# Output projection of an encoder block: another order of two products, and four instructions tied behind others

## The chip, the cores and the metric

The kernel runs on one core of a Trainium2 chip. A core has five engines that run side by side, each through its own queue in order: TensorE (PE, matrix products, with its weight loads listed as PEld), VectorE (DVE), ScalarE (ACT), GpSimd (POOL) and SyncE (SP). DMAs are issued from the queues of SP, POOL and ACT. Semaphores hold an instruction back until what it reads or overwrites is ready; what stands behind it in the same queue waits with it. The metric is the time of one execution on the device in microseconds (us); shorter is better.

## The reference: one encoder block in float32

The block has 512 tokens of width 1024. Three mixers (a bidirectional mLSTM, neighbourhood attention, cross attention into 256 memory tokens) are merged by sigmoid gates; then follow the output projection with its residual, and a convolutional GLU:

```python
h = rms_norm(x, mix_norm_g[l])
...
merged = g_ml * (y_ml @ w_br_ml[l]) + g_na * (y_na @ w_br_na[l]) + g_xa * (y_xa @ w_br_xa[l])
x = x + merged @ w_out[l]
x = x + conv_glu_ffn(rms_norm(x, ffn_norm_g[l]), w_ffn_up[l], w_ffn_conv[l], b_ffn_conv[l], w_ffn_down[l])
...
return rms_norm(x, final_norm_g)
```

The change lies in the line `x = x + merged @ w_out[l]`, with the sums of squares for the `rms_norm` of the line after it. `merged` is 512 x 1024 and `w_out` is 1024 x 1024.

## The kernel before

**Precision.** Every float32 operand of a product is split in two float32r tiles: ACT copies it (the high half), and DVE subtracts that copy from the source (the low half). `mm3` (L223 to L226) makes a product of three matmuls: high by high (L224), high by low (L225), low by high (L226). The third is the first that reads the low half of the left operand.

**The projection by seven products.** The projection (L1370 to L1460) cuts `merged` and `w_out` in quarters and uses a scheme with seven products instead of eight. `ORDER_O` names them in the order in which they run: p1, p2, p5, p6, p3, p7, p4. Each product has four steps k of two token halves t, so 4 x 2 x 3 = 24 matmuls of 128 x 512. The four quarters a11, a21, a12, a22 of the merged activations lie in `mg` (L1313). Some products read a quarter as it is (p1: a11, p2: a12, p4: a22), the others a quarter that was overwritten with a sum or difference: `early` (L1116) makes a21 = a21 - a22 and a11 = a21 - a11 after the last branch gate (L1367 and L1368); `operand` (L1123) makes the two sums for p3 (L1129 and L1130).

`operand` converts one left operand: it takes a unit (one of 15 wide buffers, `NU`), copies to the high half on ACT (L1132) and subtracts for the low half on DVE (L1136). Operands of a later product are converted at step k = 1 of the product before it (L1439).

`o_raw` (L1214) loads the right operand of a product in two halves by SP's queue, from `wout` or from `tout`, where sums of quarters of the weights were put earlier. `o_split` (L1229) converts each half: high half on ACT (L1234), low half on DVE (L1235). p6 and p7 (places 3 and 5, `RING_O`) use the three small buffers that the stream of all weights (L160, split at L184 and L185) goes through; the others use units.

**Sums of the products.** A product fills two PSUM banks, and there are two such pairs, used in turn (`wide`, L1375): a product can start once the product two places before it has been read. The reading is `add` in `wide_adder` (L1173):

- p1: ACT copies it into Q (L1180).
- p2: DVE writes p2 + Q into cell (0, 0) of x (L1182), and `residual` (L1169) issues a DMA from POOL's queue that adds the rows of the input to the cell in place (L1171).
- p5: ACT copies it into the cells (0, 1) and (1, 1) (L1186), and each gets its residual by such a DMA.
- p6: Q = p6 + Q (L1189). p3: added to cell (0, 1) (L1191). p7: Q = Q - p7 (L1193). p4: added to cell (1, 0) at the end (L1163).
- With no name and a cell, Q is added to the cell or subtracted from it (L1175).

A cell is two tiles of 128 tokens by 512 columns: cell (0, 0) is the first column half of tokens 0 to 255, cell (0, 1) the second column half of the same tokens.

**What comes after.** `squares` (L1197) makes a sum of squares over half a row of a token tile on ACT (L1199). `normed` (L1387) takes the mean of two of them (L1209, DVE), the power on POOL (L1204), and scales the rows (L1395, ACT). `turn` (L1403) transposes the scaled rows on PE (L1410); its call for tokens 0 to 255 stands at step 2 of p4, and its results, split at L230 and L231, feed the up projection of the GLU.

**What sets the order.** The loop at L1433 writes the program down; the list `todo` (L1424) names the step of a product at which each of the reading parts is written. From this a planner makes the queue of each engine: it keeps the written order as a priority, but puts an instruction that it thinks ready ahead of one that it thinks not ready yet, by its own cost model. `tc.issue_after(ins)` ties what is written within it behind `ins` on the engine of `ins`.

Of the kernel before, what the change touches and what calls it, by code (L numbers as in the profile page):

```python
# [11 lines left out]
F32 = mybir.dt.float32  # L12
F32R = mybir.dt.float32r
AF = mybir.ActivationFunctionType
ALU = mybir.AluOpType
# [3 lines left out]
S = 512  # L19
D = 1024  # L20
# [5 lines left out]
HF = FT // 2  # L26
TK = 6
ORDER = ("p1", "p5", "p6", "p3", "p7", "p2", "p4")
ORDER_O = ("p1", "p2", "p5", "p6", "p3", "p7", "p4")
RING_O = (3, 5)  # L30
OBL = [(n, hf) for n in ORDER_O for hf in range(2)]
NU = 15
# [70 lines left out]
def hybrid_block(ctx, tc, xg, xT, xtok, memT, wflat, wout, wdn, vecs, gbias, nabias, out):  # L103
    nc = tc.nc
    V, A, G, PE, SY = nc.vector, nc.scalar, nc.gpsimd, nc.tensor, nc.sync
# [17 lines left out]
    def unit(dt=F32):  # L123
        return up.tile([P, UNIT], dt, tag="unit", name=nm("u"))

    def scr(n=512):
        return sp.tile([P, S], F32, tag="scr", name=nm("s"))[:, :n]

    def tiny(n):
        return tp.tile([P, 32], F32, tag="tiny", name=nm("y"), bufs=12)[:, :n]  # L130
# [18 lines left out]
    st = {"raw": 0, "split": 0, "last": BINDEX[("ua", 0)][0] - 1}  # L149
# [148 lines left out]
    for i in range(2):  # L298
        t = cp.tile([P, 514], F32, name=f"pad{i}")
# [812 lines left out]
    def quads(pair, nk):  # L1112
        v = [u[:, :nk * S].rearrange("p (k s) -> p k s", k=nk) for u in pair]
        return v[0][:, :, :HS], v[0][:, :, HS:], v[1][:, :, :HS], v[1][:, :, HS:]

    def early(q, i):  # L1116
        a11, a21, a12, a22 = q
        if i == 0:
            V.tensor_tensor(a21, a21, a22, op=ALU.subtract)
        else:  # L1120
            V.tensor_tensor(a11, a21, a11, op=ALU.subtract)

    def operand(name, q, nk, scale=1.0):  # L1123
        a11, a21, a12, a22 = q
        u = unit(F32R)
        h, l = u[:, :nk * HS], u[:, 1024:1024 + nk * HS]
        r3 = lambda t: t.rearrange("p (k s) -> p k s", s=HS)
        if name == "p3":
            V.tensor_tensor(a21, a22, a11, op=ALU.add)  # L1129
            V.tensor_tensor(a11, a12, a11, op=ALU.add)  # L1130
        src = {"p1": a11, "p5": a21, "p6": a11, "p3": a11, "p7": a21, "p2": a12, "p4": a22}[name]
        A.activation(r3(h), src, AF.Copy, scale=scale)  # L1132
        if scale == 1.0:
            V.tensor_tensor(r3(l), src, r3(h).bitcast(F32), op=ALU.subtract)  # L1134
        else:
            V.scalar_tensor_tensor(r3(l), src, scale, r3(h).bitcast(F32), op0=ALU.mult, op1=ALU.subtract)  # L1136
        return h, l
# [4 lines left out]
    def cells(c):  # L1142
        return xtu[c[0]][:, :2 * D].rearrange("p (t n) -> p t n", t=2)[:, :, c[1] * S:(c[1] + 1) * S]
# [23 lines left out]
    def wide_adder(banks, Q):  # L1167
# [26 lines left out]

        return add

    def squares(t, n, c0, c1):  # L1197
        s = tiny(1)
        A.activation(scr(c1 - c0), xt[t][:, c0:c1], AF.Square, scale=D ** -0.5, accum_out=s)  # L1199
        n.append(s)  # L1200
# [11 lines left out]
    oraw, osp, oops, opair = [], [], {}, []  # L1212

    def o_raw(n):  # L1214
        while len(oraw) < min(n, len(OBL)):
            name, hf = OBL[len(oraw)]
            src, q = {"p1": (wout, B11), "p5": (tout, T1), "p6": (tout, T2), "p3": (wout, B22), "p7": (tout, T3),
                      "p2": (wout, B21), "p4": (tout, T4)}[name]
            n_ = ORDER_O.index(name)
            if n_ in RING_O:  # L1220
# [8 lines left out]
    def o_split(n):  # L1229
        while len(osp) < min(n, len(OBL)):  # L1230
            r = oraw[len(osp)]
            u = unit(F32R)
            h, l = u[:, :2 * S], u[:, 2 * S:4 * S]
            A.activation(h, r, AF.Copy)  # L1234
            V.tensor_tensor(l, r, h.bitcast(F32), op=ALU.subtract)  # L1235
            osp.append((h, l))

    gens = []
# [29 lines left out]
    for f in range(4):  # L1268
        ps = paced(("o", f), RN if f else RB)
        t = scr()  # L1270
# [31 lines left out]
    for f in range(4):  # L1302
        ps = paced(("naq", f), RN)
        V.tensor_tensor(nq[:, f * S:(f + 1) * S].rearrange("p (b r c) -> p b r c", r=ROWS, b=4), rv(ps), rv(rb),
                        op=ALU.mult)
# [15 lines left out]
    for br in range(3):  # L1321
# [19 lines left out]
        for fp in range(4):  # L1341
# [7 lines left out]
            if br == 2:  # L1349
                if fp == 2:  # L1350
                    mq = quads(mg, 4)
# [31 lines left out]
    add = wide_adder(obank, Qo)  # L1383
    part = [[] for _ in range(NT)]
    zs = {}

    def normed(t):  # L1387
        col = power(mean(part[t]))
        zs[t] = []
        for hf in range(2):  # L1390
            z = tp.tile([P, S], F32, tag="H", name=nm("z"), bufs=4)
            if t > 1 and hf:
                V.tensor_scalar(z, xt[t][:, hf * S:(hf + 1) * S], col, None, op0=ALU.mult)
            else:
                A.activation(z, xt[t][:, hf * S:(hf + 1) * S], AF.Copy, scale=col)  # L1395
            zs[t].append(z)

    def features():
        h2 = [unit(F32R) for _ in range(4)]
        HH.extend(h2[k // 4 * 2][:, (k % 4) * S:(k % 4 + 1) * S] for k in range(KT))  # L1400
        HL.extend(h2[k // 4 * 2 + 1][:, (k % 4) * S:(k % 4 + 1) * S] for k in range(KT))
# [14 lines left out]
    xtu = [unit(), unit()]  # L1416
    xt = [xtu[t // 2][:, t % 2 * D:(t % 2 + 1) * D] for t in range(NT)]
    SY.dma_start(cells((1, 0)), xtok[2 * P:, :S].rearrange("(t p) n -> p t n", p=P))
    oops["p2"] = operand("p2", mq, 4, 0.5)
    early(mq, 0)  # L1420
    oops["p5"] = operand("p5", mq, 4, 0.5)
    early(mq, 1)
    todo = {}
    for name, k, fn in (  # L1424
            ("p2", 1, lambda: add("p1")), ("p5", 1, lambda: add("p2")), ("p6", 1, lambda: add("p5")),
            ("p3", 1, lambda: add("p6")), ("p3", 3, lambda: [squares(t, part[t], 0, S) for t in range(2)]),
            ("p7", 0, lambda: (add("p3"), add("", (0, 1)), [squares(t, part[t], S, D) for t in range(2)])),
            ("p7", 1, lambda: [normed(t) for t in range(2)]),
            ("p4", 0, lambda: (add("p7"), add("", (1, 0)))), ("p4", 1, lambda: add("", (1, 1))),
            ("p4", 2, lambda: (features(), turn(0), [squares(t, part[t], S, D) for t in range(2, 4)]))):  # L1430
        todo.setdefault((name, k), []).append(fn)
    ua0 = BINDEX[("ua", 0)][0]
    for n, name in enumerate(ORDER_O):  # L1433
        obank[name] = wide()
        for k in range(4):
            if k % 2 == 0:
                o_raw(2 * n + k // 2 + 8)
                o_split(2 * n + k // 2 + 5)
            if k == 1 and n + 1 < len(ORDER_O) and ORDER_O[n + 1] not in oops:  # L1439
                oops[ORDER_O[n + 1]] = operand(ORDER_O[n + 1], mq, 4, 0.5)  # L1440
            if name == "p3" and k == 1:
                st["last"] = len(BLOCKS) - 1
                ahead_to(ua0 + 2, ua0 - 1)
            if (name, k) == ("p7", 3):
                ahead_to(ua0 + 2, ua0)
            if (name, k) == ("p4", 1):
                ahead_to(ua0 + 2, ua0 + 1)
            for fn in todo.pop((name, k), ()):
                fn()
            (h, l), (wh, wl) = oops[name], osp[2 * n + k // 2]  # L1450
            cs = slice(k % 2 * S, (k % 2 + 1) * S)
            for t in range(2):
                q = slice(k * HS + t * P, k * HS + (t + 1) * P)
                mm3(obank[name][:, t * S:(t + 1) * S], h[:, q], l[:, q], wh[:, cs], wl[:, cs], k == 0, k == 3)
# [141 lines left out]
    add = adder(banks, Q)  # L1596
    part = [[] for _ in range(NT)]
# [193 lines left out]
```

## Time and profile before

| | us |
|---|---|
| median of three runs | 864.83 |
| lowest, highest | 864.46, 866.22 |
| the profiled execution | 866.81 |
| its span, first to last instruction | 865.0 |
| granted TensorE clock over the span, share of full | 0.995 |
| projection: first matmul of p1 | 460.58 |
| first matmul of p2, p5, p6 | 466.02, 471.46, 476.90 |
| first matmul of p3 | 489.30 |
| transposes of tokens 0 to 255 begin | 505.49 |
| first matmul of the up projection | 510.01 |

All rows shown are from one profiled execution. A row of a timeline gives start, duration, engine, line, operation, what it writes and reads, how many were merged, and in brackets the idle time before it with the instruction that ended it. A tile's name has its buffer number left out: `u` is a unit, `at` the two banks of a product, `mm` a single bank, `xtok` the input by tokens, `s` and `y` small scratch tiles, `z` the scaled rows. A matmul's duration overlaps with that of the next; the pace is read from the starts. The page's slices are 865.0 / 40 = 21.6 us long.

### The profile page before, as it was taken

To read this page: it belongs to the slowest core of one execution; us is meant where nothing else is said; L and a number is where in the kernel's file an instruction comes from. 1 tells how busy PE (TensorE), PEld (TensorE's weight loads), DVE (VectorE), ACT (ScalarE), POOL (GpSimd) and SP (SyncE) were. 2 spreads that over 40 slices of the span, in tenths; PEclk is the share of its full clock that TensorE was granted. 3 is DMA by queue.
4 is the path that set the end of the run, shared out by engine and by line. 5 is a ranking of instruction groups with operands and counts; after the bars stand their busy time and mean duration, and the time that the engine had idled before them with its cause. 6 is when DMAs were issued, how large, how long until landed. Compare 5 with 4: busy or idle time off the path is not lost.

```text
span 865.0 us, 12105 instructions
## 1 busy us (share of the span) xinstructions
PE 850.6 (98%) x4175; PEld 719.1 (83%) x4175; DVE 622.9 (72%) x1277; ACT 481.1 (56%) x988; POOL 132.7 (15%) x245
## 2 busy tenths in 40 slices
PE   9999999999999999999999699999999999999996
PEld 7898889988888888888888588888888888888885
DVE  7774698987467758898759577475658575695684
ACT  7563467774455658888735555343434444463463
POOL 0101100010146470700000110021112010001101
PEclk9999999999999999999999899999999999999999
DMA  8233542594674353534533714578669582478952
GB/s 278 85 113 116 191 157 74 167 279 140 195 194 115 106 166 115 159 110 140 204 129 127 192 69 161 184 236 323 223 214 365 190 269 91 134 240 272 367 177 99
DMA packets 53982, 155.00 MB, mean 179 GB/s; under 512 B 6872, under 2 KB 11992, under 8 KB 53344
## 3 DMA queue, kind: packets, MB, share of 16 engines
q1 hardware_dynamic: 30912, 101.37, 34.3%
q0 software_dynamic: 22576, 52.46, 20.7%
q8 instruction: 33, 0.54, 0.2%
q10 hardware_dynamic: 432, 0.39, 0.1%
q14 instruction: 29, 0.24, 0.1%
HBM read 132.68 MB, written 29.90 MB: 188 GB/s over the span
## 4 chain that ended last, share of the span: by engine, by line
PE 96%; DMA 1%; DVE 1%; issue 1%; ACT 0%; POOLq 0%; DVEq 0%; ACTq 0%
PE mm L224 25%; PE mm L225 25%; PE mm L226 25%; PE at L224 5%; PE at L226 5%; PE at L225 5%; DMA u<-xtok 1%; PE at L990 1%; PE at L971 1%; PE at L952 0%; PE at L953 0%; PE at L773 0%; PE at L821 0%; DVE u L1235 0%; PE at L1078 0%
## 5 line engine op out<-in xcount | busy, mean ns | idle before, releaser
L224 PE MATMUL mm<-u,wh 128*128 128x512 f32 (+1 forms) x859 | 330.3, 385 | 0.1
L225 PE MATMUL mm<-u,wh 128*128 128x512 f32 (+1 forms) x859 | 327.9, 382 | 0.0
L226 PE MATMUL mm<-u,wl 128*128 128x512 f32 (+1 forms) x859 | 327.7, 382 | 0.0
L184 ACT ACTIVATE wh<-wr 128x512 fp32r<-128x512 f32 (+2 forms) x240 | 149.8, 628 | 237.0 <-PE mm L225 201.1
L185 DVE TENSOR_TENSOR wl<-wr,wh 128x512 fp32r<-128x512 f32 (+2 forms) x242 | 164.2, 683 | 86.1 <-ACT wh L184 85.5
L226 PEld LDWEIGHTS mm<-u,wl 128*128 128x128 f32 x859 | 161.5, 188 | 31.4
L225 PEld LDWEIGHTS mm<-u,wh 128*128 128x128 f32 x859 | 161.8, 188 | 30.6 <-DVE u L231 0.4
L224 PEld LDWEIGHTS mm<-u,wh 128*128 128x128 f32 x859 | 161.4, 188 | 30.0 <-ACT u L230 0.4
L548 POOL DMA_DIRECT2D u<-nav_d x128 | 62.7, 522 | 56.0 <-PE at L990 22.3
L225 PE MATMUL at<-wl,u 128*128 128x512 f32 (+2 forms) x130 | 43.9, 338 | 0.0
L226 PE MATMUL at<-wh,u 128*128 128x512 f32 (+2 forms) x130 | 43.8, 337 | 0.0
L224 PE MATMUL at<-wh,u 128*128 128x512 f32 (+2 forms) x130 | 43.7, 337 | 0.0
L1132 ACT ACTIVATE u<-u 128x1024 fp32r<-128x1024 f32 (+1 forms) x28 | 27.7, 998 | 28.7 <-PE mm L226 9.0
L224 PE MATMUL at<-u,u 128*128 128x512 f32 x80 | 32.3, 404 | 6.8 <-ACT u L1132 6.8
L1573 DVE TENSOR_TENSOR u<-mm,s 128x512 f32<-128x512 f32 x22 | 15.2, 690 | 25.1 <-PE mm L226 23.6
L1134 DVE TENSOR_TENSOR u<-u,u 128x1024 fp32r<-128x1024 f32 (+1 forms) x21 | 23.7, 1134 | 13.0 <-ACT u L1132 12.8
L226 PE MATMUL at<-u,u 128*128 128x512 f32 x80 | 32.0, 400 | 0.0
L225 PE MATMUL at<-u,u 128*128 128x512 f32 x80 | 31.8, 398 | 0.0
L225 PE MATMUL mm<-wl,u 128*128 128x512 f32 x80 | 31.2, 390 | 0.0
L226 PE MATMUL mm<-wh,u 128*128 128x512 f32 x80 | 31.1, 389 | 0.0
L224 PE MATMUL mm<-wh,u 128*128 128x512 f32 x80 | 31.0, 390 | 0.0
L1481 POOL DMA_DIRECT2D tsp<-u x22 | 15.6, 711 | 96.3 <-ACT u L1476 89.8
(365 smaller groups left out, 1335.9 us busy)
## 6 DMA issues: line engine op xcount, KB each, us to landing
wr<-wflat SPq DMA_DIRECT2D x117, 512.0 KB, 3.5
u<-wdn POOLq DMA_DIRECT2D x11, 1024.0 KB, 7.9
tsp<-u POOLq DMA_DIRECT2D x22, 512.0 KB, 6.5
u<-tsp POOLq DMA_DIRECT2D x10, 1024.0 KB, 8.1
tdn<-u POOLq DMA_DIRECT2D x11, 512.0 KB, 5.9
tout<-wout POOLq DMA_DIRECT2D x4, 1024.0 KB, 9.6
nab<-nabias SPq DMA_DIRECT2D x16, 256.0 KB, 2.8
u<-nav_d POOLq DMA_DIRECT2D x128, 32.0 KB, 2.6
```

The source lines that it names most:

```text
L184: A.activation(h[:, u:v], src, AF.Copy)
L185: V.tensor_tensor(l[:, u:v], src, h[:, u:v].bitcast(F32), op=ALU.subtract)
L224: PE.matmul(ps, lh, rh, start=start, stop=False)
L225: PE.matmul(ps, lh, rl, start=False, stop=False)
L226: st["mm"] = PE.matmul(ps, ll, rh, start=False, stop=stop).ins
L548: G.dma_start(vw[r * 32:(r + 1) * 32, i * 256:(i + 1) * 256], nav_v[hf, r, CW[b]:CW[b] + 32, hp * 256:(hp + 1) * 256])
L971: PE.transpose(pt[:, j * P:(j + 1) * P], sm[:, j * P:(j + 1) * P], ident)
L990: PE.matmul(py[:, bl * 256:(bl + 1) * 256], vw[:, c:c + P], pp[bl][:, hf * 256:(hf + 1) * 256], start=hf == 0, stop=hf == 1)
L1132: A.activation(r3(h), src, AF.Copy, scale=scale)
L1134: V.tensor_tensor(r3(l), src, r3(h).bitcast(F32), op=ALU.subtract)
L1481: G.dma_start(tsp[:, x, :, ks].rearrange("q p n -> p q n"), hl[0][:, x])
L1573: V.tensor_tensor(ur, pu, c, op=ALU.mult)
```

## The change

The products run in the order p1, p5, p2, p6, p3, p7, p4. The operand of p5 is now written before that of p2, and the reading of the sums follows the new order: p1 is read at step 1 of p5, p5 at step 1 of p2, p2 at step 1 of p6.

The operand of p4 is written at step 2 of p3; before, it was written at step 1 of p7.

The subtraction of Q from cell (0, 1) (L1175) moves from step 0 of p7 to step 3 of p3, so it is now written ahead of the addition of p3 to the same cell, and is tied on DVE behind the last low half that `o_split` has written by then: that of the second half of p4's weights. The sums of squares over cell (0, 0) stay at step 3 of p3 and are tied on ACT behind the last conversion that `operand` has written: that of p4.

```diff
-ORDER_O = ("p1", "p2", "p5", "p6", "p3", "p7", "p4")
+ORDER_O = ("p1", "p5", "p2", "p6", "p3", "p7", "p4")
...
-        A.activation(r3(h), src, AF.Copy, scale=scale)
+        st["oh"] = A.activation(r3(h), src, AF.Copy, scale=scale).ins
...
+    def after(ins, fn):
+        with tc.issue_after(ins):
+            fn()
+
...
-            V.tensor_tensor(l, r, h.bitcast(F32), op=ALU.subtract)
+            st["ol"] = V.tensor_tensor(l, r, h.bitcast(F32), op=ALU.subtract).ins
...
-    oops["p2"] = operand("p2", mq, 4, 0.5)
     early(mq, 0)
     oops["p5"] = operand("p5", mq, 4, 0.5)
+    oops["p2"] = operand("p2", mq, 4, 0.5)
     early(mq, 1)
...
-            ("p2", 1, lambda: add("p1")), ("p5", 1, lambda: add("p2")), ("p6", 1, lambda: add("p5")),
-            ("p3", 1, lambda: add("p6")), ("p3", 3, lambda: [squares(t, part[t], 0, S) for t in range(2)]),
-            ("p7", 0, lambda: (add("p3"), add("", (0, 1)), [squares(t, part[t], S, D) for t in range(2)])),
+            ("p5", 1, lambda: add("p1")), ("p2", 1, lambda: add("p5")), ("p6", 1, lambda: add("p2")),
+            ("p3", 1, lambda: add("p6")), ("p3", 3, lambda: after(st["ol"], lambda: add("", (0, 1)))),
+            ("p3", 3, lambda: after(st["oh"], lambda: [squares(t, part[t], 0, S) for t in range(2)])),
+            ("p7", 0, lambda: (add("p3"), [squares(t, part[t], S, D) for t in range(2)])),
...
+            if (name, k) == ("p3", 2):
+                oops["p4"] = operand("p4", mq, 4, 0.5)
```

## The prediction

> **What bounds the kernel now.** I read the page's shares and slices first, then the list of who waited for whom, the chain of waits around the one dent, and the timelines of ACT, DVE and PE there.
>
> ```profile
> PE 850.6 (98%) x4175; PEld 719.1 (83%) x4175; DVE 622.9 (72%) x1277; ACT 481.1 (56%) x988; POOL 132.7 (15%) x245
> PE   9999999999999999999999699999999999999996
> PEclk9999999999999999999999899999999999999999
> ...
> PE at L224 <- ACT u L1132: 6.8, 1, 6.8
> PE at L253 <- PEq L1784: 0.8, 1, 0.8
> ```
>
> TensorE sets the time: only its idle time and its slow clock can be won. Between the ends there is one dent, slice 23 (476 to 497 us), and the only wait of more than 0.8 us is a single one of 6.8 us on an operand conversion (L1132). The chain says what held that up (start us, length, what):
>
> ```profile
> 473.59 1.23 DVE u L1182
> ...
> 475.39 11.55 DMA u<-xtok
> ...
> 487.50 0.80 ACT s L1199 x3
> ```
>
> A residual transfer (L1171) runs for 11.55 us, square sums (L1199) read what it adds to, and p3's conversion stands behind them on ACT's in-order queue. ACT's and DVE's timelines show that the conversion itself had been free to run:
>
> ```profile
> 478.64 1.93 ACT L1186 ACTIVATE u<-at 128x1024 f32<-128x1024 f32 x2
> 486.97 0.63 ACT L1199 ACTIVATE s<-u 128x512 f32<-128x512 f32 x1 [6.40 <-DMA u<-xtok]
> 488.21 1.04 ACT L1132 ACTIVATE u<-u 128x1024 fp32r<-128x1024 f32 x1
> ...
> 478.86 1.22 DVE L1130 TENSOR_TENSOR u<-u,u 128x1024 f32<-128x1024 f32 x1
> 479.99 0.68 DVE L185 TENSOR_TENSOR wl<-wr,wh 128x512 fp32r<-128x512 f32 x1
> 489.28 1.23 DVE L1136 SCALAR_TENSOR_TENSOR u<-u,u 128x1024 fp32r<-128x1024 f32 x1 [8.61 <-ACT u L1132]
> ```
>
> Its input (L1130) was complete at 480.08 and ACT was free at 480.57; it started at 488.21. The square sums are wanted only two products later.
>
> **What the stall costs.** PE's timeline gives the pace before it, the gap, and the slow restart (the last row is one of the windows view):
>
> ```profile
> 466.02 0.39 PE L224 MATMUL at<-u,u 128*128 128x512 f32 x1
> 466.47 0.39 PE L226 MATMUL at<-u,u 128*128 128x512 f32 x1
> ...
> 471.46 0.39 PE L224 MATMUL at<-u,u 128*128 128x512 f32 x1
> ...
> 482.11 0.39 PE L226 MATMUL at<-u,u 128*128 128x512 f32 x1
> 489.30 0.79 PE L224 MATMUL at<-u,u 128*128 128x512 f32 x1 [6.80 <-ACT u L1132]
> ...
> 493.71 0.59 PE L224 MATMUL at<-u,u 128*128 128x512 f32 x1
> 494.14 0.39 PE L225 MATMUL at<-u,u 128*128 128x512 f32 x1
> 490.00:494.00 4.00, 3.96 (x10) 2.76 (x9) 4.00 (x5) 4.00 (x6) 0.00 (x0) 0.50 0.40 136
> ```
>
> A product is 24 matmuls, 466.02 to 471.46: 0.2267 us each. After the last matmul of p6 (482.11) p3 was due at 482.34 and began at 489.30: 6.96 us. Then ten matmuls take 4.84 us instead of 2.27, since the granted clock is 0.50 from 490 to 494 (the windows row gives length, busy time of PE, PEld, DVE, ACT and POOL, clock, DMA share, GB/s): 2.57 us more. The eleventh, due at 484.61, starts at 494.14. **The stall is worth 9.53 us**, and what follows p3 is again a full PE.
>
> [...]
>
> **The change, part by part.**
>
> *Square sums behind p4's conversion, p4's operand at p3's third step.* ACT no longer meets the transfer before the conversions of p3, p7 and p4. What is late next for p3? Its low half (DVE, 1.22 us) would end at 480.57 + 1.04 + 1.22 = 482.83, and the third matmul, the first to read it, is due at 482.34 + 0.45 = 482.79. Moreover L1182 (1.23 us at 473.59), which reads p2's banks, now comes after the third product and leaves DVE's queue ahead of L1129 and L1130, so they come about 1.1 us sooner. I charge nothing. Gain: 9.53 us.
>
> *p5 second, p2 third.* Both operands need the last branch gate, and p5's also a subtraction on DVE (L1119):
>
> ```profile
> 462.23 1.06 ACT L1132 ACTIVATE u<-u 128x1024 fp32r<-128x1024 f32 x1 [7.44 <-DVE u L1368]
> 463.49 1.07 ACT L1132 ACTIVATE u<-u 128x1024 fp32r<-128x1024 f32 x1 [0.20 <-DVE u L1119]
> 462.23 1.23 DVE L1119 TENSOR_TENSOR u<-u,u 128x1024 f32<-128x1024 f32 x1
> 463.37 1.22 DVE L1136 SCALAR_TENSOR_TENSOR u<-u,u 128x1024 fp32r<-128x1024 f32 x1
> 464.51 1.22 DVE L1121 TENSOR_TENSOR u<-u 128x1024 f32<-128x1024 f32 x1
> 465.64 1.22 DVE L1136 SCALAR_TENSOR_TENSOR u<-u,u 128x1024 fp32r<-128x1024 f32 x1
> ```
>
> p2's conversion is ready first and, in this order, p5's low half ends at 466.86. PE starts the second product at 466.02 and reads the low half with its third matmul at 466.47. If the planner keeps the order, PE waits 466.92 - 466.47 = 0.45 us; if it puts p5's low half ahead of L1121, nothing. Ends 0 and 0.45; I take 0.45, since the rows show p5's conversion ending (464.56) just after DVE came free (464.51). The weight loads change places on SP's queue with the same bytes; second and third weights are split long before their products.
>
> *The transfers.* p5's two copies (L1186, 1.93 us) now follow the second product, at 471.9, so the two transfers for its cells are issued at about 472.9 and 474.1; p2's cell follows L1182 after 476.9, so at about 478.4, the last in POOL's queue instead of the first.
>
> ```profile
> 475.39 1.26 POOL L1171 DMA_DIRECT2D u<-xtok  x1 [110.08 <-DVE u L1182]
> 479.95 2.40 POOL L1171 DMA_DIRECT2D u<-xtok  x2 [3.31 <-PE at L226]
> DMA to landing us min/median/max: 10.2/11.6/11.8
> ```
>
> They take 10.2 to 11.8 us, so the cells of p5 are there by 486 and that of p2 at 488.6 to 490.2. Nothing for PE hangs on POOL's queue in between (its next work is the powers, L1204).
>
> *The subtraction (L1175) behind the last weight split, and the added waits.* On DVE, behind it stand p3's add (L1191, which frees the banks that p4 needs), and then the means; on ACT, behind the square sums, stand the second square sums and the normalised rows that PE transposes. So the question is when these are done:
>
> ```profile
> 462.23:480.67 18.44, 18.44 (x83) 15.28 (x82) 18.40 (x17) 13.83 (x15) 1.97 (x2) 1.00 0.54 172
> 489.28:501.02 11.74, 11.68 (x41) 9.01 (x42) 10.39 (x10) 5.75 (x7) 0.00 (x0) 0.79 0.20 60
> ...
> 499.80 1.22 DVE L1175 TENSOR_TENSOR u<-u,u 128x1024 f32<-128x1024 f32 x1
> 503.04 2.57 ACT L1395 ACTIVATE z<-u,y 128x512 f32<-128x512 f32 x4 [0.65 <-POOL y L1204]
> 505.49 1.91 PE L1410 MATMUL mm<-ident,z 128*128 128x128 f32 x16
> ```
>
> DVE is busy without a break to 480.67 (18.40 of 18.44 us) and has 10.39 us more to do up to the end of L1175: with the stall gone, 491.1. The add L1191 is among it and is not early: p3 ends at 487.8 and p4 wants the banks at 493.7. In the trace of before the last normalised row (505.61) comes 4.59 us after L1175's end (501.02), and 0.12 us after the transposes' start, without harm. PE now reaches the transposes at 482.34 + 60 x 0.2267 + 0.45 = 496.4. So L1175 may end at 491.9; the first square sums (1.24 us, 486.97 to 488.21 above) after a transfer landed by 490.2 are through at 491.4. If two more weight splits of 0.68 us (L185) come in between, L1175 ends at 492.4, 0.5 late. Ends 0 and 0.5, and up to 2 if a transfer lands that much later; I take 0.2, near the nine operations that the rows do show.
>
> **Sum.** -9.53 + 0.45 + 0.2 = -8.9 us. The profiled execution took 866.81 us (span 865.0 and 1.81 around it), so 857.9. It ran 1.98 us over the median of the three runs (864.83); on that median: **855.9 us**.
>
> **Rivals.**
>
> *Part of the wait comes back at the transposes.* p2's cell is now the last of three transfers, in a stretch where the DMA engines are full (the last column but one is their busy share):
>
> ```profile
> 475.00:482.00 7.00, 7.00 (x33) 5.79 (x32) 5.64 (x6) 3.43 (x5) 3.30 (x3) 1.00 0.93 261
> 482.00:490.00 8.00, 1.20 (x5) 0.58 (x3) 0.72 (x1) 3.03 (x6) 0.35 (x1) 0.83 1.08 247
> ```
>
> Landing at 493 instead of 490 delays the square sums and PE by some 2.5 us, with the 2.57 us restart at most: 857.3 to 861. For it: those shares. Against: the same bytes in the same stretch, and two of the transfers start earlier than before.
>
> *The conversion is still held.* ACT's queue can put something else that waits for a transfer ahead of p3's conversion; a split (L184) waited there already:
>
> ```profile
> 477.58 1.15 ACT L184 ACTIVATE wh<-wr 128x512 fp32r<-128x512 f32 x2 [2.13 <-DMA wr<-wflat]
> wr<-wflat SPq DMA_DIRECT2D x1, 512.0 KB, 8.6
> ```
>
> The next load (issued 477.10, landing 485.7 by the second row) with its split of 1.15 would let the conversion go at 486.9 instead of 488.2: 863.5, within 861 to 866. Against: with L1182 gone from before it, the conversion is ready earlier than that load.
>
> *Slower: transfers issued under a full DVE start only when DVE falls idle.* DVE would run on to 488.6 (491.1 less L1175 and L1191), the transfers then take 11.8 us to 500.4, L1175 and L1191 end at 502.8, and p4 waits for its banks from 493.7: 9.1 us and 2.57 of restart against 9.1 saved, 867.4. It loses from a landing after 497.8, 25 us after issue. Against it: the transfer of 475.39 was issued under a DVE busy to 480.67 and landed at 486.94, in 11.55 us; the other two, with DVE idle after 480.67, took as long. [...]
>
> **How the numbers follow.** About 0.2% (1.7 us) is what a measurement of this kernel can tell from none: 863.1 to 866.6 is the same. Forecast 0.64 (855.0 to 857.3), wait at the transposes 0.20, still held 0.10 (nearly all of it the same, a little faster), slower 0.06 (one part in six within the same). Faster 0.86, same 0.09, slower 0.05. The range 854.8 to 861.0 covers the first two: full gain with no new wait and 0.5 us of scatter below, the second's far end above.
>
> **What would show it.** Right: no ACT wait on u<-xtok ahead of p3's L1132; no PE wait over 1 us between 460 and 505; slice 23 a 9 in PE and PEclk; a PE wait of about 0.4 us after 466.02; transposes at about 496.5. Wrong: a wait of PE on L1395 or L1191 (transfers late), an L184 or L1234 waiting on a DMA ahead of p3's conversion (still held), POOL's transfers landing over 20 us after issue.

## The result and the profile after

| | before | after |
|---|---|---|
| median, us | 864.78 (864.46 to 866.22, 4 runs) | 859.14 (858.79 to 859.69, 4 runs) |
| ratio | 1 | 0.9932 (0.9915 to 0.9949) |
| the profiled execution, us | 866.81 | 858.97 |
| first matmul of the up projection, us | 510.01 | 501.88 |

Two single executions far above all others, 1738.94 us of the run e4 below and 1219.79 us of the kernel before beside it, are left out of the medians and intervals.

The change saves 5.64 us between the medians and 7.84 us between the two profiled executions. The forecast was 8.9 on both. Line numbers from L1197 on are a few higher now: the square sums are L1203, the halves of the projection's weights L1238 and L1239, the scaled rows L1399, the transposes L1414, the means L1213, the powers L1208.

The page of the changed kernel (busy time and two rows of its 40 slices), then its list of what PE waited for (in total, times, longest):

```profile
PE 848.3 (99%) x4175; PEld 716.8 (84%) x4175; DVE 622.6 (73%) x1277; ACT 480.2 (56%) x988; POOL 133.0 (16%) x245
...
PE   9999999999999999999999999999999999999996
...
PEclk9999999999999999999999999999999999999999
```

```profile
PE mm L1414 <- ACT z L1399: 0.9, 1, 0.9
...
PE mm L224 <- ACT wh L184: 0.3, 1, 0.3
```

The dent of slice 23 is gone, in PE and in its clock; the wait of 6.8 us for p3's conversion has left the list, and a new one of 0.9 us stands at the transposes. ACT's timeline shows what took the old one's place:

```profile
463.49 2.01 ACT L1132 ACTIVATE u<-u 128x1024 fp32r<-128x1024 f32 x2 [8.70 <-DVE u L1119]
...
478.54 1.15 ACT L184 ACTIVATE wh<-wr 128x512 fp32r<-128x512 f32 x2 [2.73 <-DMA wr<-wflat]
479.60 1.04 ACT L1132 ACTIVATE u<-u 128x1024 fp32r<-128x1024 f32 x1
...
486.46 1.05 ACT L1132 ACTIVATE u<-u 128x1024 fp32r<-128x1024 f32 x1
491.64 0.63 ACT L1203 ACTIVATE s<-u 128x512 f32<-128x512 f32 x1 [4.13 <-DMA u<-xtok]
...
492.88 0.62 ACT L184 ACTIVATE wh<-wr 128x512 fp32r<-128x512 f32 x1
...
495.42 2.56 ACT L1399 ACTIVATE z<-u,y 128x512 f32<-128x512 f32 x4 [0.70 <-POOL y L1208]
```

p3's conversion runs at 479.60 instead of 488.21. The square sums still wait for a transfer, 4.13 us long, but only after the last operand's conversion (486.46), when nothing behind them is due at once. Behind them, though, stand the scaled rows, and the first transposes find only part of these. PE's timeline there, and POOL's for the transfers:

```profile
495.72 0.39 PE L226 MATMUL at<-u,u 128*128 128x512 f32 x1
496.20 0.33 PE L1414 MATMUL mm<-ident,z 128*128 128x128 f32 x1
497.43 1.86 PE L1414 MATMUL mm<-ident,z 128*128 128x128 f32 x15 [0.89 <-ACT z L1399]
```

```profile
473.31 2.48 POOL L1171 DMA_DIRECT2D u<-xtok  x2 [106.27 <-DMA wr<-tout]
479.82 1.18 POOL L1171 DMA_DIRECT2D u<-xtok  x1 [4.03 <-DVE u L1182]
```

Before, the up projection came 510.01 - 505.49 = 4.52 us after the first transpose. Here the transposes were due at 495.95 (495.72 and one pace of 0.23), so the up projection at 500.47; it came at 501.88, 1.41 us late. Together that is -9.53 + 1.41 = -8.12 us. The first matmul of p1 starts at 460.58 in both executions, and the up projection 8.13 us earlier in the second. The third wait of the list, 0.3 us at L224, lies in the first 100 us, ahead of the projection, and moves nothing in it. The last 0.3 us between the two spans are lost behind the up projection: from there to the end it takes 355.0 us before and 355.3 after, but 355.3 also in a second execution of the kernel before (e1), so this isn't put down to the change.

### The profile page after: what moved, and what is told of

Same layout as the page of the kernel before. It is cut to its first block, busy times and chain, and to the rows that moved or that the text cites. A ratio compares the mean times of both kernels' runs of the same rounds, so it can differ in the third digit from the quotient of the medians.

```text
span 857.2 us, 12114 instructions
## 1 busy us (share of the span) xinstructions
PE 848.3 (99%) x4175; PEld 716.8 (84%) x4175; DVE 622.6 (73%) x1277; ACT 480.2 (56%) x988; POOL 133.0 (16%) x245
## 4 chain that ended last, share of the span: by engine, by line
PE 94%; DVE 2%; DMA 2%; ACT 1%; issue 1%; POOL 0%; SPq 0%; POOLq 0%
PE mm L224 25%; PE mm L225 25%; PE mm L226 25%; PE at L225 4%; PE at L226 4%; PE at L224 4%; DMA u<-xtok 1%; PE at L990 1%; PE at L971 1%; DVE u L1239 1%; DMA wr<-wflat 0%; PE at L952 0%; PE at L953 0%; PE at L773 0%; PE at L821 0%
## 5 line engine op out<-in xcount | busy, mean ns | idle before, releaser
L224 PE MATMUL mm<-u,wh 128*128 128x512 f32 (+1 forms) x859 | 330.1, 385 | 0.4 <-ACT wh L184 0.3
L184 ACT ACTIVATE wh<-wr 128x512 fp32r<-128x512 f32 (+2 forms) x240 | 149.8, 628 | 236.6 <-PE mm L225 198.8
L185 DVE TENSOR_TENSOR wl<-wr,wh 128x512 fp32r<-128x512 f32 (+2 forms) x242 | 164.2, 683 | 84.2 <-ACT wh L184 83.5
L224 PEld LDWEIGHTS mm<-u,wh 128*128 128x128 f32 x859 | 161.3, 188 | 30.9 <-ACT wh L184 0.7
L224 PE MATMUL at<-wh,u 128*128 128x512 f32 (+2 forms) x130 | 43.7, 337 | 0.0
L1134 DVE TENSOR_TENSOR u<-u,u 128x1024 fp32r<-128x1024 f32 (+1 forms) x21 | 23.7, 1134 | 13.6 <-ACT u L1132 13.5
L224 PE MATMUL at<-u,u 128*128 128x512 f32 x80 | 31.2, 390 | 0.0
L226 PE MATMUL at<-u,u 128*128 128x512 f32 x80 | 31.1, 389 | 0.0
L225 PE MATMUL at<-u,u 128*128 128x512 f32 x80 | 31.1, 389 | 0.0
L224 PE MATMUL mm<-wh,u 128*128 128x512 f32 x80 | 31.0, 390 | 0.0
```

Of the source, the lines that this page charges most:

```text
L184: A.activation(h[:, u:v], src, AF.Copy)
L185: V.tensor_tensor(l[:, u:v], src, h[:, u:v].bitcast(F32), op=ALU.subtract)
L224: PE.matmul(ps, lh, rh, start=start, stop=False)
L225: PE.matmul(ps, lh, rl, start=False, stop=False)
L226: st["mm"] = PE.matmul(ps, ll, rh, start=False, stop=stop).ins
```

## The experiments

The question was which of the parts of the change (order, tie of the square sums, tie of the subtraction, p4's operand written earlier) does the work, and where 3.2 us of the forecast gain went. Theory: p3's conversion is held by the square sums, these by one transfer, and the stall is as long as that transfer happens to be. Rivals: the new order does it; another wait or ACT itself holds p3; the transfer, now last, comes back at the transposes. The ties hold three instructions of the program, one subtraction and two square sums (each of these is two rows of ACT).

Medians in us; the kernel before ran beside each group of four on the same chip. The last column is from the one profiled execution of each run: the time from the first matmul of p1 to the first matmul of the up projection. It is 49.43 in the kernel before and 41.30 in the changed one, and 39.88 where nothing waits in between. p1 itself starts between 459.90 and 460.89, so a row of one execution can be compared with a row of another only from that matmul.

| run | median (lowest to highest) | ratio to before (95%) | p1 to up projection |
|---|---|---|---|
| e1: before once more | 864.72 (863.50 to 869.10) | 1.0004 (0.9991 to 1.0018) | 47.11 |
| e2: old order, both ties | 858.54 (858.15 to 858.78) | 0.9924 (0.9908 to 0.9940) | 41.35 |
| e3: new order, no tie | 864.40 (863.10 to 865.82) | 0.9992 (0.9981 to 1.0002) | 46.20 |
| e8: new order, square sums tied | 857.52 (856.46 to 857.73) | 0.9914 (0.9896 to 0.9931) | 39.88 |
| e9: the changed kernel once more | 858.60 (857.52 to 859.75) | 0.9933 (0.9920 to 0.9946) | 41.09 |
| e13: e8 once more | 857.87 (857.61 to 859.98) | 0.9930 (0.9916 to 0.9943) | 40.36 |
| e10: e8, p2's sum read earlier | 863.00 (861.44 to 864.63) | 0.9980 (0.9971 to 0.9990) | 45.26 |
| e11: changed, one transfer left out | 858.14 (857.31 to 859.48) | 0.9927 (0.9914 to 0.9939) | 40.48 |
| e12: before, same transfer left out | 859.17 (858.40 to 860.18) | 0.9939 (0.9921 to 0.9957) | 41.56 |
| e4: old order, square sums tied, p4's operand early | 859.92 (859.21 to 862.77) | 0.9951 (0.9933 to 0.9969) | 41.85 |
| e14: old order, square sums tied, nothing else | 858.74 (858.48 to 859.51) | 0.9936 (0.9918 to 0.9953) | 41.04 |
| e6: changed, two pieces of weights split earlier | 860.25 (859.99 to 860.59) | 0.9951 (0.9931 to 0.9970) | 41.84 |

### e1: how long is the stall in another execution?

No edit: the kernel before, with a second profile.

> The kernel before, once more, for the 2 us between the profiled pair (865.0 to 857.2 us of span, 7.8 us) and the medians (864.78 to 859.14 us, 5.6 us). Theory A: the stall at p3 is as long as the residual transfer happens to take, and the profiled execution had a long one (11.55 us, 9.53 us lost); another execution near the median shows a transfer of some 9 to 10 us, a stall of 7 to 8 us in all, and p3's first matmul near 487.5 instead of 489.30. Theory B: the stall is always about 9.5 us, and the 2 us lie elsewhere in the execution: p3 starts at 489.3 again and the first matmul of the up projection at 510.0, with the difference before 460 or after 510.

Timelines of ACT and PE, the windows view around the restart (its columns as in the prediction), and the residual transfers' landing times:

```profile
483.10 0.63 ACT L1199 ACTIVATE s<-u 128x512 f32<-128x512 f32 x1 [3.99 <-DMA u<-xtok]
```

```profile
481.44 0.39 PE L226 MATMUL at<-u,u 128*128 128x512 f32 x1
485.43 0.80 PE L224 MATMUL at<-u,u 128*128 128x512 f32 x1 [3.61 <-ACT u L1132]
```

```profile
490.00:492.00 2.00, 2.00 (x7) 1.52 (x6) 2.00 (x3) 1.15 (x3) 0.00 (x0) 0.50 0.23 90
492.00:494.00 2.00, 2.00 (x10) 1.65 (x9) 0.31 (x1) 0.00 (x0) 0.00 (x0) 0.98 0.00 0
```

```profile
DMA to landing us min/median/max: 8.4/9.4/11.0
```

The same program, the same held conversion, but the transfer took 8.4 us instead of 11.55. p3 was due at 481.67 and began at 485.43: 3.76 us idle. Transposes began at 502.50; 60 matmuls of 0.2267 after 481.67 they were due at 495.27. So this execution lost 7.23 us (3.76 idle, 3.47 at the half clock), and the one that the prediction read lost 9.55 by the same sum (505.49 less 495.94). Without their losses the two come to 856.8 and 857.3: **most of the surplus of the profiled execution was stall** (2.3 of the 2.75 us between the two), as theory A has it, with a transfer even shorter than the 9 to 10 us that it named. An estimate from these two: the median execution, at 864.8, loses about 7.7 us.

### e3 and e2: the order alone, and the ties alone

e3, against the kernel before:

```diff
-ORDER_O = ("p1", "p2", "p5", "p6", "p3", "p7", "p4")
+ORDER_O = ("p1", "p5", "p2", "p6", "p3", "p7", "p4")
...
-    oops["p2"] = operand("p2", mq, 4, 0.5)
...
+    oops["p2"] = operand("p2", mq, 4, 0.5)
...
-            ("p2", 1, lambda: add("p1")), ("p5", 1, lambda: add("p2")), ("p6", 1, lambda: add("p5")),
+            ("p5", 1, lambda: add("p1")), ("p2", 1, lambda: add("p5")), ("p6", 1, lambda: add("p2")),
```

> The new order of the products without the ties; p4's operand at step 1 of p7 again. In ACT's queue the square sums now stand behind p3's and p7's conversions and ahead of p4's only. Theory A (the ties matter): the transfer of p2's cell lands near 491.6, p4's conversion runs near 493, its low half and behind it on DVE the add L1191 and the subtraction come after 494, p4's banks are free near 497 instead of 493.2, and the time is 3 to 6 us over the changed kernel, 862 to 865. Rival (the order alone is enough, since p3's conversion is free): within 1 us of the changed kernel, 858.5 to 860.

Its timelines of ACT, DVE and PE:

```profile
491.00 0.63 ACT L1203 ACTIVATE s<-u 128x512 f32<-128x512 f32 x1 [4.86 <-DMA u<-xtok]
...
492.24 1.04 ACT L1132 ACTIVATE u<-u 128x1024 fp32r<-128x1024 f32 x1
```

```profile
493.31 1.23 DVE L1136 SCALAR_TENSOR_TENSOR u<-u,u 128x1024 fp32r<-128x1024 f32 x1 [5.92 <-ACT u L1132]
...
495.06 1.22 DVE L1191 TENSOR_TENSOR u<-at,u 128x1024 f32<-128x1024 f32 x1
```

```profile
496.42 0.47 PE L224 MATMUL at<-u,u 128*128 128x512 f32 x1 [3.32 <-DVE u L1191]
```

p3 is free in the new order, but the square sums now stand ahead of p4's conversion. That comes at 492.24, its low half at 493.31, and behind the low half on DVE stands p3's addition, whose banks p4 needs. The stall has moved by two products, and the time is that of before, as theory A expected; the rival, that the order alone is enough, is out.

e2 keeps the old order and takes the rest of the change:

```diff
-            ("p3", 1, lambda: add("p6")), ("p3", 3, lambda: [squares(t, part[t], 0, S) for t in range(2)]),
-            ("p7", 0, lambda: (add("p3"), add("", (0, 1)), [squares(t, part[t], S, D) for t in range(2)])),
+            ("p3", 1, lambda: add("p6")), ("p3", 3, lambda: after(st["ol"], lambda: add("", (0, 1)))),
+            ("p3", 3, lambda: after(st["oh"], lambda: [squares(t, part[t], 0, S) for t in range(2)])),
+            ("p7", 0, lambda: (add("p3"), [squares(t, part[t], S, D) for t in range(2)])),
...
+            if (name, k) == ("p3", 2):
+                oops["p4"] = operand("p4", mq, 4, 0.5)
```

> The two ties and the early operand of p4 as in the change, the products in the old order. Theory A (the square sums ahead of p3's conversion on ACT are the whole stall): it goes here too; p3 starts on time near 482.3. p2's cell is then early (lands near 487), but the two cells of p5 are issued at 479.95 and land at 490 to 492, and DVE's subtraction L1175 and add L1191 wait for them: the normalised rows come near 499.3 instead of 498.0, PE waits some 3 us at p4 and the transposes, and the time is 1 to 2.5 us over the changed kernel, 860 to 861.5. Rival (the new order is what frees p3's conversion, by taking L1182 out of DVE's queue and the copies L1186 off ACT's): p3's conversion is still held and the time is near that of before, 864.

It comes below the range of either theory, at the changed kernel's time: p3 is not held, as theory A has it, but the late landings cost less than expected. The ties alone bring the whole gain; the order brings nothing beside them. In the old order p2's transfer starts first, and the tied square sums (485.11) meet no wait at all; what DVE waits for is a later landing, 0.69 us at the tied subtraction. PE still waits 1.3 us at the transposes.

### e12: the transfer as the cause

```diff
             if name == "p2":
                 V.tensor_tensor(cells((0, 0)), ps, Q[0], op=ALU.add)
-                residual((0, 0))
```

> The kernel before, with the residual of cell (0, 0) left out: its output lacks the input's rows in that cell. Nothing else is changed, neither the order of the products nor any tie. Theory (p3's conversion is held by the square sums, and these by that one transfer): the square sums run by 479 without a wait, p3 starts at its turn, slice 23 is full, and the time is 856.5 to 858.5, as low as the changed kernel without the same transfer (858.1). Rival (ACT itself is too full around 480 for p3's conversion, or another transfer holds it): the dent stays at 3 us or more and the time is above 861.

Its lines behind the one left out are one lower than in the kernel before: L1198 are the square sums, L1208 the means, L1203 the powers, L1192 is p7's sum. ACT's and DVE's timelines and PE's waits:

```profile
475.50 0.62 ACT L1198 ACTIVATE s<-u 128x512 f32<-128x512 f32 x1
...
480.99 1.06 ACT L1132 ACTIVATE u<-u 128x1024 fp32r<-128x1024 f32 x1
```

```profile
491.76 1.22 DVE L1175 TENSOR_TENSOR u<-u,u 128x1024 f32<-128x1024 f32 x1
...
493.77 0.21 DVE L1208 TENSOR_SCALAR y<-y,y 128x1 f32<-128x1 f32 x1 [0.19 <-ACT s L1198]
494.12 1.22 DVE L1192 TENSOR_TENSOR u<-u,at 128x1024 f32<-128x1024 f32 x1
495.25 0.21 DVE L1208 TENSOR_SCALAR y<-y,y 128x1 f32<-128x1 f32 x1
```

```profile
PE mm L1409 <- ACT z L1394: 0.9, 1, 0.9
...
PE at L226 <- DVE u L1136: 0.3, 1, 0.3
```

With the transfer gone and not one tie added, the stall of 6.8 us is gone: the transfer was its cause, and the rival of a full ACT is out. The size was expected too low by 0.7 us. The first square sums no longer wait for anything, yet PE still waits 0.9 us at the transposes. L1175 comes as late as 491.76 on a DVE that has been busy without a break. Then p7's sum (L1192) stands between the two means (L1208), so that the second mean comes 0.9 us after its square sum has ended (494.36), and the rows that wait for the power on POOL behind it start 1.59 us after that mean has ended, where the first pair started 0.70 us after its own (more on that in the last section). The second pair of scaled rows is late by both. That wait is thus not the transfer's alone.

### e4 and e14: how little of the change is enough

e14, the whole edit beside the helper `after` and the two remembered instructions:

```diff
-            ("p3", 1, lambda: add("p6")), ("p3", 3, lambda: [squares(t, part[t], 0, S) for t in range(2)]),
+            ("p3", 1, lambda: add("p6")),
+            ("p3", 3, lambda: after(st["oh"], lambda: [squares(t, part[t], 0, S) for t in range(2)])),
```

> The old order, the square sums tied only behind the conversion that is written last at that place, that of p7; p4's operand is written where it was, at p7's step 1, and stands behind the square sums. Theory (only what stands behind the waiting square sums on ACT matters, and when it is due): the square sums start when the transfer of 475 lands, at 485 to 487; p4's conversion follows by 488.5 and is due at 493, so nothing waits: 857.2 to 858.8, the same as with p4's operand moved. Rival (p4's conversion has to be moved ahead too): PE waits 1 us or more at p4, 860 or more.

ACT's timeline, and PE's longest wait:

```profile
484.77 0.63 ACT L1203 ACTIVATE s<-u 128x512 f32<-128x512 f32 x1
...
486.00 1.06 ACT L1132 ACTIVATE u<-u 128x1024 fp32r<-128x1024 f32 x1
```

```profile
PE mm L1414 <- ACT z L1399: 0.9, 1, 0.9
```

As expected at p4; the 0.9 us at the transposes stay. The square sums stand behind p7's conversion; by the time ACT is through with that and a weight half (484.77), the transfer of 475.16 has landed, and p4's conversion follows at 486.00, long before its turn. This one tie gives the changed kernel's time within the intervals.

e4 is e14 with p4's operand written at step 2 of p3, as in the change, so that the square sums stand behind that conversion.

> The old order of products, p4's operand written early, the square sums tied behind its conversion; the subtraction L1175 stands behind p3's addition as before. Theory (the tie of the square sums is the whole gain): p3 is not held, L1175 no longer meets the last landing (0.69 us of DVE's wait in the run with both ties), transposes at about 496, 857.2 to 858.6. Rival (the tie of the subtraction is needed as well, because DVE's p3 addition would come too late for p4's banks or the second square sums): a wait of PE of 1 us or more at p4 or at the transposes and 860 or more.

Measured 859.92, between the theory's range and the rival's, with PE waiting 1.2 us at the transposes and not at p4; the interval overlaps with those of e14 and e2. But e14 lacks the tie of the subtraction too and stays within the theory's range, so the missing tie isn't the reason. The profiled execution of e4 (860.19) shows where it lost against that of e14 (858.54). Some 0.6 us go at p3, whose low half is late: its conversion stands behind a weight split (L184) whose load landed 0.6 us later than in e14, counted from p1. Another 0.2 go at the transposes; p3's addition had to wait 0.42 us on DVE for a landing. And 1.1 us go near 790 us, far behind the projection, where PE waits for a late split of weights (L1540). Of all profiles only those of e4, e6 and e13 show that loss, and e8, the same kernel as e13, does not. Whether the early operand has a part in any of this isn't shown.

### e8 and e13: without the tie of the subtraction

Against the changed kernel:

```diff
-            ("p3", 1, lambda: add("p6")), ("p3", 3, lambda: after(st["ol"], lambda: add("", (0, 1)))),
+            ("p3", 1, lambda: add("p6")),
...
-            ("p7", 0, lambda: (add("p3"), [squares(t, part[t], S, D) for t in range(2)])),
+            ("p7", 0, lambda: (add("p3"), add("", (0, 1)), [squares(t, part[t], S, D) for t in range(2)])),
```

> The change without the tie of the subtraction: L1175 back at step 0 of p7, behind p3's add; the square sums stay tied behind p4's conversion. If p2's transfer (landing near 491.6) sets the transposes, as the changed kernel's chain of waits says, L1175 at 491 to 492.4 instead of 488.9 to 490.0 costs nothing: within 0.5 us of the changed kernel, 858.6 to 859.6. If DVE's queue sets them, the normalised rows come 0.6 us later or more: 859.7 to 861.

In e8's profiled execution PE has no wait at the transposes. Its timelines of ACT and PE:

```profile
489.76 0.63 ACT L1203 ACTIVATE s<-u 128x512 f32<-128x512 f32 x1 [3.53 <-DMA u<-xtok]
```

```profile
495.29 1.91 PE L1414 MATMUL mm<-ident,z 128*128 128x128 f32 x16
```

The time of 857.52 lies below both ranges. The transfer landed by 489.76, not 491.62; 0.66 us of that is only that p1 started at 459.92 instead of 460.58. To part the tie from the luck of a landing, the same kernel and the changed one ran again beside each other:

> The new order with the square sums tied and the subtraction L1175 back behind p3's add, once more. Theory A: within 0.7 us of the changed kernel on the same chip. Theory B: 1 to 2 us faster than it.

> The changed kernel once more, on one chip with the kernels beside it. Theory A (what is left over the floor is the wait of the transposes for p2's residual transfer, and it varies with that transfer): the time lies 0.5 to 2 us over a kernel of the same order whose square sums read nothing that a DMA adds to, and where its transfer lands about 1 us earlier than the 491.6 us of the first profile, the transposes wait about 1 us less. Theory B (the tie of the subtraction costs the 1.6 us between 859.14 and the 857.52 us of the kernel without it): 1 to 2 us over the repeat of that kernel, whatever the transfer does.

The median of e13 is 0.73 us lower, with overlapping intervals: just over theory A's 0.7 and under theory B's 1. The two profiled executions differ by the same 0.73 us from p1 to the up projection. Of these, 0.38 are a landing: the square sums start at 491.37 in e13 and at 491.38 in e9, but that is 30.48 and 30.86 us after p1. The rest is how soon the scaled rows follow on ACT, e13 first:

```profile
494.78 2.57 ACT L1399 ACTIVATE z<-u,y 128x512 f32<-128x512 f32 x4 [0.33 <-POOL y L1208]
```

```profile
495.16 2.56 ACT L1399 ACTIVATE z<-u,y 128x512 f32<-128x512 f32 x4 [0.70 <-POOL y L1208]
```

They wait for the first power (L1208), which takes 0.57 us in e13 and 0.94 in e9 (both powers together 1.16 and 1.48), where an L185 follows the first mean on DVE and runs beside the power. The three profiles with the subtraction tied in the new order (the changed kernel, e9, e11) have the long power, the three with the square sums alone tied (e8, e13, e10) the short one. **The subtraction's tie brings nothing**, and may cost these 0.4 us. This version, without it, had the lowest medians of all, 857.52 and 857.87; against the changed kernel its lead is not settled.

### e10 and e11: the late transfer

e10 is e13 with p2's sum read one step earlier, so that its transfer starts sooner:

```diff
-            ("p5", 1, lambda: add("p1")), ("p2", 1, lambda: add("p5")), ("p6", 1, lambda: add("p2")),
+            ("p5", 1, lambda: add("p1")), ("p2", 1, lambda: add("p5")), ("p6", 0, lambda: add("p2")),
```

> As the kernel before, and p2's sum (L1182) written at step 0 of p6, ahead of the sum L1130 that p3's operand reads. Its transfer is issued 1.1 us earlier, and p3's low half has to follow 1.4 us later, at about 482. Theory A: the transfer lands 1 us earlier and the transposes never wait; 0 to 1 us under the repeat of the kernel without this, 856.5 to 857.5. Theory B: the transposes hang on DVE's queue, and the time stays within 0.3 us of that kernel; if p3's low half is late, PE waits at p3 for up to 0.5 us and it is slower by that.

Timelines of POOL, ACT, DVE and PE, and a row of the windows view:

```profile
478.39 1.18 POOL L1171 DMA_DIRECT2D u<-xtok  x1 [2.90 <-DVE u L1182]
```

```profile
492.03 0.63 ACT L1203 ACTIVATE s<-u 128x512 f32<-128x512 f32 x1 [6.91 <-DMA u<-xtok]
...
493.27 1.14 ACT L184 ACTIVATE wh<-wr 128x512 fp32r<-128x512 f32 x2
```

```profile
493.92 0.69 DVE L185 TENSOR_TENSOR wl<-wr,wh 128x512 fp32r<-128x512 f32 x1 [4.34 <-ACT wh L184]
494.53 1.22 DVE L1175 TENSOR_TENSOR u<-u,u 128x1024 f32<-128x1024 f32 x1
```

```profile
498.22 0.33 PE L1414 MATMUL mm<-ident,z 128*128 128x128 f32 x1 [2.42 <-ACT z L1399]
499.44 2.74 PE L1414 MATMUL mm<-ident,z 128*128 128x128 f32 x15 [0.90 <-ACT z L1399]
```

```profile
501.00:502.00 1.00, 1.00 (x7) 1.00 (x6) 0.28 (x1) 1.00 (x4) 0.00 (x0) 0.50 0.00 0
```

The expectation of 856.5 to 857.5 fell. Counted from p1, the transfer did start 1.1 us earlier than in e13, but it took 13.6 us and landed 1.3 us later. And the planner now put both weight splits (L184) behind the waiting square sums; DVE sat 4.34 us before the low half of the first (L185), with L1175 queued behind it. It is the fault of before in a new place: ready work behind a waiting instruction, this time on two engines.

e11 takes the transfer out of the changed kernel:

```diff
                 V.tensor_tensor(cells((0, 0)), ps, Q[0], op=ALU.add)
-                residual((0, 0))
```

> The changed kernel without the residual transfer of cell (0, 0): that part of x lacks its residual, and the square sums over it read nothing that a DMA adds to. Theory A: the transposes start on time, no wait of PE between 460 and 505 over 0.3 us, and the time is the floor of this order: 0.5 to 2 us under the changed kernel, 856 to 857.5. Theory B (DVE's queue with its tied subtraction sets the transposes): no change beyond 0.3 us.

The wait at the transposes falls from 0.9 to 0.4 us. From p1 to the up projection it takes 40.48 us, 0.6 less than in e9 and 0.8 less than in the first profile of the changed kernel: that is what the late transfer costs there. Between the medians it is 0.46, with overlapping intervals. Neither theory is met: the time is over A's range, and the difference over B's 0.3. The up projection is still 0.6 us later than with no wait at all (39.88); about 0.4 of that is the first power, 0.95 us long beside an L185 as in e9.

### e6: the split between the square sums

Against the changed kernel:

```diff
-            if (name, k) == ("p7", 3):
-                ahead_to(ua0 + 2, ua0)
-            if (name, k) == ("p4", 1):
+            if (name, k) == ("p3", 3):
                 ahead_to(ua0 + 2, ua0 + 1)
```

> The changed kernel, with the splits of the two next pieces of weights (L184 on ACT, L185 on DVE) written ahead of the square sums, so that none stands between them. Theory (DVE's queue is the next limit behind the transfer, so moving its work only exchanges one wait for another): four L185 of 0.68 us stand ahead of L1175, which starts at about 491, the second square sums at about 494, transposes within 0.6 us of the changed kernel's: 858 to 859.5. Rival (the split between the square sums is what keeps the last 1.4 us from the transposes): 857.0 to 857.6.

DVE's timeline and PE's longest wait:

```profile
488.12 2.49 DVE L185 TENSOR_TENSOR wl<-wr,wh 128x512 fp32r<-128x512 f32 x4
490.52 1.22 DVE L1175 TENSOR_TENSOR u<-u,u 128x1024 f32<-128x1024 f32 x1
491.85 1.23 DVE L1191 TENSOR_TENSOR u<-at,u 128x1024 f32<-128x1024 f32 x1
```

```profile
PE mm L1414 <- ACT z L1399: 1.4, 1, 1.4
```

The rival is out: with no split between the square sums the time rises to 860.25, 0.75 above the range of the theory. The four low halves go ahead of L1175 and L1191, and the second square sums, which read what these write, come no sooner (493.11, or 32.80 us after p1; 32.83 in the changed kernel). Then p7's sum stands between the two means, as in e12 and e14 and not in the changed kernel, and the second pair of scaled rows, behind the second power, starts at 496.92, 1.59 us after the second mean has ended. A version that ties that sum behind the second mean was not tried. From p1 to the up projection e6 takes 0.5 to 0.8 us more than the changed kernel's two profiles. Another 1.1 us of its profiled execution go near 790 us, as in e4 and e13; whether they belong to the edit isn't shown.

## Why the prediction came out as it did

- **The stall.** Right in its mechanism: e12 takes away the transfer, e14 one place in ACT's queue, and with either p3 starts at its turn. The term, 9.53 us, is right for the execution that was read. What failed is the step behind the sum, "on that median": it took the 1.98 us by which that execution lay above the median for an offset that the change leaves alone. e1 shows that most of it was stall, and so part of what the change removes. The gain on the median is smaller by about that.
- **p5's low half, 0.45 us.** It didn't come. (The rows give 466.86 for its end, so 0.39; no row shows the 466.92 of the sum.) The planner put L1121 ahead of both low halves; the lower end held, and PE ran on at its pace.
- **The transposes, 0.2 us.** Measured 1.41, outside the ends of 0 and 0.5 but within the "up to 2" for a late landing. p2's cell was issued at 479.82 rather than 478.4, since L1182 came behind p3's sum on DVE, and landed at 491.6 rather than by 490.2; and the wait ran through ACT, where a weight split stood between the square sums, and through the long first power on POOL, not through L1175, which was done by 490.1. This is the rival at the transposes in small: its place and cause, without the restart. About 0.6 to 0.8 us are the transfer's (e11), and about 0.4 the power's, which the prediction did not price.
- **The end.** 0.3 us behind the up projection were not in the sum; they vary between executions of one kernel.
- **Sum.** The 3.24 us between 855.9 and 859.14 are the 1.98 of the median, 1.2 of the transposes, 0.3 of the end, less 0.45 for p5, and 0.2 by which the median after lies above its profiled execution. The likeliest case's own range, 855.0 to 857.3, missed; the whole range, to 861.0, held the time. That it did is in part luck: its upper part was there for a late transfer with a restart of the clock, and more than half of the miss came from the median, for which it left no room.
- **Still held.** An L184 did wait for a load ahead of p3's conversion (478.54), but that load landed in time, as argued.
- **Slower.** The transfer issued at 479.82 landed after 11.8 us although DVE was busy for 7.86 of the 8 us from 482 and for 3.02 of the next 4: it isn't held until DVE is idle.
- **The edits costed at nothing.** The order (e2, e3) and the subtraction's tie (e8, e13) bring no gain that these runs can show; p4's early operand is needed in the new order, where the square sums wait until 491 and in e3 hold p4's conversion, and not in the old one (e14).

## What to carry to other kernels

Look on each in-order engine for an instruction that waits for a transfer while ready work stands behind it, and tie it behind that work, as far as its own result allows; here one such tie was worth as much as the whole change, and moving the transfer instead only moved the wait. Before a gain read from one profiled execution is taken off a median, see whether what sets that execution apart is the very stall to be removed: a second profile of the same kernel tells. When the stall is gone, read the engines behind the waiting one (here DVE and POOL ahead of the transposes) before trying to start the transfer sooner. Compare rows of two executions from a common event and not from the start of the span.

## What the runs showed of the hardware

**An accumulating transfer of a cell has no fixed price.** p2's transfer took 8.4 us in one execution of the kernel before and 11.55 in another; in e10, issued 1.1 us earlier than in e13 (counted from p1), it took 13.6 us against 11.2 and landed 1.3 us later. What sets it, these runs don't show.

**The half clock comes after less than the 6.96 us of the first profile, and costs no less.** After 3.76 us idle (e1) the clock was at 0.50 until 492 and 3.47 us were lost; after 6.96 us it was 2.57. From the mean clock of its windows (0.80 from 487.0 to 487.5 and 0.87 from 494.0 to 494.5 in the first profile, 0.81 from 484 to 486 and 0.98 from 492 to 494 in e1, 0.50 between), the half clock is put at 487.3 to 494.1 in the first profile and at 485.2 to 492.1 in e1: it lasted 6.8 us in both, and the loss differs because p3 began 2.0 us into it in the first and 0.2 us into it in e1. In e3, after 3.47 us idle, and in e10 it lasted 3.4 us and set in 0.45 and 0.8 us after PE was at work again (e3: 0.97 from 495 to 497, 0.50 to 499, 0.68 to 501; e10: 0.62 from 500 to 501, 0.50 to 503, 0.67 to 504). In e10 it followed gaps of 2.42 and 0.90 us with a single transpose of 0.33 us between them, neither of them as long by itself as the 3.47 us of e3; the gap of 1.4 us in e6 left the clock alone (1.00 from 496 to 502).

**A power on POOL takes 0.54 to about 0.6 us beside L1193 or an idle DVE, and up to 1.48 beside other work of DVE.** POOL's two powers and DVE's work beside them, in e2:

```profile
493.30 0.57 POOL L1208 TENSOR_TENSOR y<-y,nhalf 128x1 f32<-128x1 f32 x1 [11.97 <-DVE y L1213]
494.54 1.48 POOL L1208 TENSOR_TENSOR y<-y,nhalf 128x1 f32<-128x1 f32 x1 [0.67 <-DVE y L1213]
```

```profile
493.12 1.21 DVE L1193 TENSOR_TENSOR u<-u,at 128x1024 f32<-128x1024 f32 x1
494.38 2.36 DVE L1175 TENSOR_TENSOR u<-u,u 128x1024 f32<-128x1024 f32 x2
```

In the five profiles where L1175 runs beside the second power (e2, e4, e6, e12, e14) the rows that wait for it start 1.59 us after the second mean has ended, and in e2 1.48 of these are the power; in the three where an L185 runs beside the first (the changed kernel, e9, e11), this takes 0.94 or 0.95; beside L1193, or an idle DVE, it is 0.54 to about 0.6 (two together take 1.11 us in the kernel before, 1.16 in e8, e13 and e10). L1193 reads a PSUM bank, L1175 and L185 don't. Whether that is the reason these runs don't show: none changes it alone.
